# The output projection of a hybrid decoder layer: its weights brought in by halves of their columns, and the last attention head filled with products of two token tiles

## The chip, the cores and the metric

The kernel runs on one core of a Trainium2 chip. The metric is device microseconds of one launch. Before the change three runs gave 1188.72, 1190.84 and 1192.52 us, so the median is 1190.84 us.

## The reference, cut to what matters

One decoder layer on 1024 tokens of width 1024, in float32. Only the middle of it is touched by the change: the mixed output of the two head groups is multiplied by `w_out`, normed and added to the residual.

```python
h = rms_norm(x, norm_mix_pre)
proj = h @ w_in                                  # 2816 columns: u, v of group A; q, k, v of group B
a_out = spatial_gating(ua, va, ...)              # 4 channel groups, 256 columns
b_out = dilated_attention(qb, kb, vb, rel_bias)  # 12 heads, 768 columns
mix = concatenate([a_out, b_out])                # 1024 tokens x 1024
x = x + rms_norm(mix @ w_out, norm_mix_post)     # the part that the change touches
h = rms_norm(x, norm_ffn_pre)
g = gelu(causal_dwconv(h @ w_gate, conv_w, conv_b))
x = x + rms_norm((g * (h @ w_up)) @ w_down, norm_ffn_post)
```

## The kernel before, in words

**Products.** Nearly every matrix product is made of three: each float32 operand is split into a high part (a copy rounded to the format that TensorE takes, on ACT or DVE) and a low part (the difference, on DVE or POOL). `split(hi, lo, src, hi_eng, lo_eng)` at L71 issues the pair, and PE multiplies high by high, high by low and low by high.

**Stages.** First the projection of u, v and the v columns, then the twelve attention heads, then `mix @ w_out` for eight token tiles of 128 tokens (with the norms behind it), then the channel mixer with its gate, up and down products. The attention takes the span from about 130 us to 458 us, the eight tiles of `w_out` from 458 to 545 us.

**One head.** Head h has four groups g of two query tiles. PE makes the scores `s` (L538, L539), DVE adds the bias and takes the row's extreme (`row`, `nm`, L542), ACT takes the exponential (L547), DVE the reciprocal (`rz`, L549), POOL scales the row (L550), PE transposes it (`pt`, L570), ACT and DVE split the transpose (`pth` L574, `ptl` L575), and PE multiplies it by v (`o`, L592). ACT and DVE then put the result into `mix` (`ot` L604, L605). The scores of the next group are issued ahead of the products of this one. Between these steps PE gets fill work from a queue, so many matmuls at each place by the table `FILL_AT`: the q and k projection of the head after next (`qk`, L498), and in the last head (h = 11), which has no head after it, 42 matmuls of `w_out` for token tile 0 (`y`, L649).

**Who orders what.** PE and SP (which issues the DMAs) run in the order in which the code is written. ACT, DVE and POOL get their order from a scheduler at build time. All five run strictly in that order: an instruction that waits holds up all behind it on its engine.

**w_out.** `load_wo(k)` (L624) loads one block of 128 rows by 1024 columns (512 KB) into a raw buffer and splits it into `woh` and `wol`, 512 columns at a time. There are two raw buffers (pool `rp`), which the q and k weights of the heads use as well, so the load of block k+2 waits until block k is split. The tables `WO_HI` and `WO_LO` give the engines by block, and `WO_AT` the place: blocks 0 to 3 in head 10, at groups 0 and 2, blocks 4 and 5 at its group 3, blocks 6 and 7 behind it. `mix_split` (L633) splits the 128 columns of one token tile out of each of the eight `mix` tiles into `ms`, the stationary operand of the `w_out` products. Tile 0 is split in head 10.

**Behind the heads.** At L1112 the last block of `mix` is split for tile 0, its last six matmuls follow, and `wout_end` (L719) takes the sum of squares from both halves of `y`, norms, adds the residual `xb` and norms again. `h2_trans` (L756) then transposes the result of a tile on PE (`hT`, L747), which stands in PE's order behind all of the next tile's matmuls. The banks of PSUM: S three, P two, O one, D two. The two halves of `y` for tile 0 take both banks of D.

Of the kernel before, what the change touches and what calls it, by code (L numbers as in the profile page):

```python
# [52 lines left out]
WQK_HI = 'aa'  # L53
WO_HI = 'dadaddda'
WO_LO = 'pppppppd'
WO_AT = {0: (0, 1), 1: (), 2: (2, 3), 3: (4, 5), 4: (6, 7)}
# [6 lines left out]
def build(tc, x, g1, g2, g3, g4, w_in, ln_g, ln_b, sp_w, sp_b, rel, w_out, w_gate, w_up,  # L63
# [25 lines left out]
    def close_pool(key):  # L89
        cms.pop(key).__exit__(None, None, None)  # L90

    with tc.manual_schedule(engines={ET.PE, ET.SP}), \
# [530 lines left out]

        def load_wo(k):  # L624
            r = raw("wo%d" % k)
            sp.dma_start(r, w_out[k * 128:(k + 1) * 128, :])
            wh = htile("woh%d" % k)
            wl = htile("wol%d" % k)
            for s in (slice(0, 512), slice(512, 1024)):
                split(wh[:, s], wl[:, s], r[:, s], ENG[WO_HI[k]], ENG[WO_LO[k]])  # L630
            WO.append((wh, wl))

# [8 lines left out]

        def wout_mm(i, ks, get):
            def mm(hf, k, j):
                def f():
                    if k == 0 and j == 0:
                        YP[i, hf] = get("y%d_%d" % (i, hf))
                    m = MS[i][1 if j == 2 else 0][:, k]
                    w = WO[k][1 if j == 1 else 0][:, hf * 512:(hf + 1) * 512]
                    pe.matmul(YP[i, hf], m, w, start=k == 0 and j == 0, stop=k == KT - 1 and j == 2)  # L649
                return f  # L650
            return [mm(hf, k, j) for k in ks for hf in range(2) for j in range(3)]

# [6 lines left out]
        for h in range(HEADS):  # L659
# [6 lines left out]
            if h == HEADS - 1:  # L666
                pump(len(fill))
                fill.extend(wout_mm(0, range(KT - 1), bD))
            for g in range(4):
# [16 lines left out]
                if g == 3 and h == HEADS - 2:  # L686
                    pump(len(fill))
                    for k in WO_AT[4]:
                        load_wo(k)
        pump(len(fill))  # L690
        last_pv()
        close_pool("ag")
        close_pool("ag2")
# [421 lines left out]
        load_xb(1)  # L1115
        for f in wout_mm(0, [KT - 1], bD):
            f()
        wout_end(0)
        mt = mix_tiles(1)
        mix_split(1, mt[0], mt[1], range(KT))  # L1120
        for c in range(1, NT):
# [7 lines left out]
            if c == 6:  # L1129
# [3 lines left out]
                hs_sums(0, 2)  # L1133
            for f in wout_mm(i, range(KT), bS if c % 2 else bD):
                f()
# [153 lines left out]
```

## Time and profile before

| | before |
|---|---|
| median of three runs | 1190.84 us (1188.72 to 1192.52) |
| the profiled execution | 1192.9 us, its span 1191.2 us |
| mean granted TensorE clock | 0.996 |
| PE busy | 1162.8 us (98% of the span), 5697 matmuls |
| DVE, ACT, POOL busy | 832.0, 593.1, 351.0 us |
| head 11's first transposes to its last product | 435.05 to 457.9 us |

Of the execution's time, 1.7 us lie outside the span. Columns of a timeline row are the start and the duration in us, the engine, the line, the operation and its operands; a bracket at the end gives the idle time of the engine just before it and who ended that. PE's rows are pipelined and overlap; what a matmul costs is read from the distance between starts.

### The profile page before, as it was taken

The numbers are of one execution on the slowest core, as the hardware profiler recorded it, in microseconds if no ns is written. First come the engines' busy times: TensorE is split into PE (matmuls) and PEld (weight loads), VectorE is DVE, ScalarE is ACT, GpSimd is POOL, SyncE is SP. The second block draws the span as 40 slices with busy tenths as digits, with TensorE's granted clock in tenths as the row PEclk, the third lists the DMA queues.
The fourth block names the chain that finished last, engine by engine and source line by source line (L and its number), as shares of the span: only waits on it lengthen the run. The fifth ranks groups of instructions, "written<-read, shape, count | busy, mean of one in ns | idle before, by whom it ended". The sixth has DMA issues, their size and how long they took to land.

```text
span 1191.2 us, 16581 instructions
## 1 busy us (share of the span) xinstructions
PE 1162.8 (98%) x5697; PEld 975.0 (82%) x5697; DVE 832.0 (70%) x1553; ACT 593.1 (50%) x1233; POOL 351.0 (29%) x356
## 2 busy tenths in 40 slices
PE   8999999999999999998999999999999999999997
PEld 5889978888888878877788888888888888888885
DVE  6842157767777775467997778767777679679666
ACT  6522157676766665467534243433434245445642
POOL 2841023333334473224133313332233310000240
PEclk9999999999999999999999999999999999999999
DMA  5314033443234341341143313333243279334337
GB/s 196 104 47 113 2 83 73 103 108 83 74 78 110 86 131 72 103 164 53 36 133 97 106 65 130 123 108 89 80 133 97 85 279 370 114 98 120 113 108 245
DMA packets 107421, 134.31 MB, mean 113 GB/s; under 512 B 30780, under 2 KB 74312, under 8 KB 107337
## 3 DMA queue, kind: packets, MB, share of 16 engines
q1 hardware_dynamic: 105030, 131.15, 36.1%
q10 hardware_dynamic: 2306, 2.10, 0.5%
q8 instruction: 45, 0.74, 0.3%
q14 instruction: 40, 0.32, 0.1%
HBM read 98.30 MB, written 35.71 MB: 113 GB/s over the span
## 4 chain that ended last, share of the span: by engine, by line
PE 82%; issue 4%; ACT 4%; POOL 4%; DVE 4%; DMA 1%; DVEq 0%; POOLq 0%; ACTq 0%; SPq 0%
PE d L1015 15%; PE qk L498 10%; PE y L649 5%; PE o L592 4%; PE pt L570 4%; PE s L538 2%; PE s L539 2%; PE v L253 2%; PE Bu L876 2%; PE v L254 2%; PE v L255 2%; PE Bu L874 2%; PE Bu L875 2%; PE Au L876 2%; PE Cu L876 2%
## 5 line engine op out<-in xcount | busy, mean ns | idle before, releaser
L1015 PE MATMUL d<-t,s 128*128 128x512 f32 x924 | 210.4, 389 | 0.8 <-DVE t L78 0.8
L1015 PEld LDWEIGHTS d<-t,s 128*128 128x128 f32 x924 | 173.2, 188 | 37.8 <-DVE t L78 1.7
L550 POOL TENSOR_SCALAR row<-row,rz 128x128 f32<-128x128 f32 (+3 forms) x96 | 72.7, 757 | 208.3 <-DVE rz L549 190.7
L547 ACT ACTIVATE row<-row,nm 128x128 f32<-128x128 f32 (+3 forms) x96 | 74.4, 775 | 49.7 <-DVE nm L542 49.5
L575 DVE TENSOR_TENSOR ptl<-pt,pth 128x512 fp32r<-128x512 f32 (+1 forms) x120 | 75.7, 634 | 20.0 <-ACT pth L574 18.7
L649 PE MATMUL y<-woh,ms 128*128 128x512 f32 x256 | 82.8, 396 | 1.0 <-POOL ms L78 0.6
L574 ACT ACTIVATE pth<-pt 128x512 fp32r<-128x512 f32 (+1 forms) x120 | 65.9, 551 | 33.3 <-PE pt L570 31.9
L498 PE MATMUL qk<-hTh,wqh 128*128 128x512 f32 x192 | 81.0, 422 | 0.0
L73 ACT ACTIVATE s<-sf 128x512 fp32r<-128x512 f32 x77 | 48.2, 626 | 63.1 <-PE d L1015 26.3
L498 PE MATMUL qk<-hTl,wqh 128*128 128x512 f32 x192 | 78.7, 410 | 0.0
L498 PE MATMUL qk<-hTh,wql 128*128 128x512 f32 x192 | 76.7, 400 | 0.0
L78 DVE TENSOR_TENSOR s<-sf,s 128x512 fp32r<-128x512 f32 x77 | 57.1, 741 | 21.1 <-ACT s L73 21.0
L570 PE MATMUL pt<-ident,row 128*128 128x128 f32 x432 | 68.3, 275 | 1.1 <-POOL row L550 1.0
L73 ACT ACTIVATE wtg<-tg 128x512 fp32r<-128x512 f32 x44 | 27.4, 632 | 81.4 <-PE Cu L876 67.8
L1030 POOL TENSOR_TENSOR x<-x,g4t 128x512 f32<-128x512 f32 x12 | 18.0, 1516 | 163.4 <-ACT n4m L1040 133.5
L927 DVE SCALAR_TENSOR_TENSOR c<-G,cols,c 128x1023 f32<-128x1023 f32 (+1 forms) x44 | 57.7, 1327 | 6.7 <-ACT c L925 6.7
L542 DVE CUSTOM_DVE_ANT_0 row<-s,bias 128x384 f32<-128x384 f32 (+2 forms) x96 | 49.9, 520 | 17.8 <-PE s L539 12.4
L824 POOL TENSOR_TENSOR tu<-wu 128x512 f32<-128x512 f32 x11 | 16.9, 1537 | 153.6 <-PE Ag L876 74.5
L73 ACT ACTIVATE wtu<-tu 128x512 fp32r<-128x512 f32 x44 | 27.6, 630 | 63.9 <-PE Cg L876 50.8
L570 PEld LDWEIGHTS pt<-ident,row 128*128 128x128 f32 x432 | 51.2, 140 | 10.0 <-POOL row L550 2.0
L649 PEld LDWEIGHTS y<-woh,ms 128*128 128x128 f32 x256 | 47.9, 188 | 11.7 <-POOL ms L78 1.0
L592 PE MATMUL o<-ptl,V 128*128 128x256 f32 x240 | 49.1, 286 | 3.7 <-DVE ptl L575 3.4
(334 smaller groups left out, 3214.1 us busy)
## 6 DMA issues: line engine op xcount, KB each, us to landing
sf<-sD SPq DMA_DIRECT2D x77, 256.0 KB, 2.9
wu<-in_w_up SPq DMA_DIRECT2D x11, 1024.0 KB, 5.1
wd<-in_w_down SPq DMA_DIRECT2D x22, 512.0 KB, 6.9
wg<-in_w_gate SPq DMA_DIRECT2D x10, 1024.0 KB, 6.5
sD<-c SPq DMA_DIRECT2D x30, 256.0 KB, 6.4
gcop<-gd SPq DMA_DIRECT2D x12, 576.0 KB, 4.8
wqk<-in_w_in SPq DMA_DIRECT2D x24, 256.0 KB, 5.8
bias<-gcop SPq DMA_DIRECT2D x12, 512.0 KB, 3.9
```

Source lines behind the costliest of these rows:

```text
L73: act.activation(hi, src, AF.Copy)
L498: pe.matmul(st[hf], w, m, start=k == 0 and j == 0, stop=k == KT - 1 and j == 2)
L547: act.activation(t[:, :w], t[:, :w], AF.Exp, bias=nm, scale=-1.0, accum_out=z)
L550: pool.tensor_scalar(t[:, :w], t[:, :w], rz, 1.0, op0=OP.mult, op1=OP.mult)
L570: pe.transpose(p[:, a * 128:(a + 1) * 128], r[:, jj * 128:(jj + 1) * 128], ident)
L574: act.activation(hi[:, :n], p[:, :n], AF.Copy)
L575: dve.tensor_sub(lo[:, :n], p[:, :n], hi.bitcast(F)[:, :n])
L592: pe.matmul(ov, v, t[:, s], start=j == 0 and x == 0, stop=x == 1 and j == 2 * g + 1, skip_group_check=True)
L649: pe.matmul(YP[i, hf], m, w, start=k == 0 and j == 0, stop=k == KT - 1 and j == 2)
L876: pe.matmul(b, wl, hh, start=False, stop=last and k == 3, skip_group_check=True)
L927: dve.scalar_tensor_tensor(c[:, d:T], g[:, 0:T - d], col(2 - d, f), c[:, d:T], op0=OP.mult, op1=OP.add)
L1015: pe.matmul(b, l, r, start=first and n in FIRST and q == 0, stop=last and n in LAST and q == 2, skip_group_check=True)
```

## The change

`w_out` is brought in by halves of 512 columns (256 KB each). `load_wo(k, hf)` loads and splits half hf of block k. The first halves stand where the whole blocks stood. The second halves are written into the last group of head 11 (blocks 0 to 3) and behind the last head's products (blocks 4 to 7), with their high parts on ACT and their low parts on DVE and POOL in turn. The 42 fill matmuls of the last head become 21 for tile 0 and 21 for tile 1, all on first halves, and so tile 1 of `mix` is split at the start of head 11 instead of behind it (the high parts on ACT, the low parts on POOL). Behind the heads follow the last block's first half for both tiles (6 matmuls), then all of the second half for tile 0 (24), its `wout_end`, and all of the second half for tile 1 (24).

```diff
-WO_HI = 'dadaddda'
-WO_LO = 'pppppppd'
+WO_HI = 'dadaddda', 'aaaaaaaa'
+WO_LO = 'pppppppd', 'dpdpdpdp'
...
-        def load_wo(k):
-            r = raw("wo%d" % k)
-            sp.dma_start(r, w_out[k * 128:(k + 1) * 128, :])
-            wh = htile("woh%d" % k)
-            wl = htile("wol%d" % k)
-            for s in (slice(0, 512), slice(512, 1024)):
-                split(wh[:, s], wl[:, s], r[:, s], ENG[WO_HI[k]], ENG[WO_LO[k]])
-            WO.append((wh, wl))
+        def load_wo(k, hf=0):
+            s = slice(hf * 512, (hf + 1) * 512)
+            r = raw("wo%d_%d" % (k, hf))
+            sp.dma_start(r[:, :512], w_out[k * 128:(k + 1) * 128, s])
+            if hf == 0:
+                WO.append((htile("woh%d" % k), htile("wol%d" % k)))
+            wh, wl = WO[k]
+            split(wh[:, s], wl[:, s], r[:, :512], ENG[WO_HI[hf][k]], ENG[WO_LO[hf][k]])
...
-        def wout_mm(i, ks, get):
+        def wout_mm(i, ks, get, hfs=(0, 1)):
...
-            return [mm(hf, k, j) for k in ks for hf in range(2) for j in range(3)]
+            return [mm(hf, k, j) for k in ks for hf in hfs for j in range(3)]
...
             if h == HEADS - 1:
                 pump(len(fill))
-                fill.extend(wout_mm(0, range(KT - 1), bD))
+                m1 = [mtile("ms1_%d" % s, R).rearrange("p (k c) -> p k c", k=KT) for s in range(2)]
+                mix_split(1, m1[0], m1[1], range(KT - 1), (act, pool))
+                for i in range(2):
+                    fill.extend(wout_mm(i, range(KT - 1), bD, (0,)))
...
+                if g == 3 and h == HEADS - 1:
+                    for k in range(4):
+                        load_wo(k, 1)
         pump(len(fill))
         last_pv()
+        for k in range(4, KT):
+            load_wo(k, 1)
...
-        for f in wout_mm(0, [KT - 1], bD):
+        mix_split(1, m1[0], m1[1], [KT - 1])
+        for i in range(2):
+            for f in wout_mm(i, [KT - 1], bD, (0,)):
+                f()
+        for f in wout_mm(0, range(KT), bS, (1,)):
             f()
         wout_end(0)
-        mt = mix_tiles(1)
-        mix_split(1, mt[0], mt[1], range(KT))
         for c in range(1, NT):
...
-            for f in wout_mm(i, range(KT), bS if c % 2 else bD):
+            for f in wout_mm(i, range(KT), (lambda nm: (bD if nm.endswith("_0") else bS)(nm)) if c == 2 else bS if c % 2 else bD, (1,) if c == 1 else (0, 1)):
                 f()
```

What the scheduler and the buffers make of it is seen in the order of the instructions. PE's own order keeps every row in its place in the last head; only the operands of the fill change. On DVE the cast of block 0 at the start of head 10, which stood behind both score rows of query tile 4, now stands right behind `ptl` of group 0, ahead of the reciprocal of query tile 3 and of those score rows. Three more places count.

The first is ACT, from the transposes of head 11's third group to the first norm of `w_out`'s result. Before:

```order
L574 ACTIVATE pth_2_2_5430<-pt_2_2_5426 128x384
L604 ACTIVATE ot_2_5447<-o_2_5408 64x256
L574 ACTIVATE pth_3_0_5455<-pt_3_0_5450 128x512
L574 ACTIVATE pth_3_1_5465<-pt_3_1_5460 128x512
L574 ACTIVATE pth_3_2_5481<-pt_3_2_5476 128x512
L574 ACTIVATE pth_3_3_5493<-pt_3_3_5489 128x384
L604 ACTIVATE ot_3_5508<-o_3_5459 64x256
L725 ACTIVATE yb_5533,ssb_5534<-y_0_5269 128x512
```

The same place after the change, where `wo_1` is a raw second half:

```order
L574 ACTIVATE pth_2_2_5430<-pt_2_2_5426 128x384
L73 ACTIVATE woh_5125<-wo_1_5527 128x512
L604 ACTIVATE ot_2_5447<-o_2_5408 64x256
L574 ACTIVATE pth_3_0_5455<-pt_3_0_5450 128x512
L574 ACTIVATE pth_3_1_5465<-pt_3_1_5460 128x512
L73 ACTIVATE woh_5131<-wo_1_5531 128x512
L73 ACTIVATE woh_5206<-wo_1_5535 128x512
L574 ACTIVATE pth_3_2_5481<-pt_3_2_5476 128x512
L574 ACTIVATE pth_3_3_5493<-pt_3_3_5489 128x384
L604 ACTIVATE ot_3_5524<-o_3_5459 64x256
L73 ACTIVATE woh_5212<-wo_1_5539 128x512
L734 ACTIVATE yb_5592,ssb_5593<-y_0_5269 128x512
```

The copies of blocks 4 (`woh_5125`), 5 (`woh_5131`) and 6 (`woh_5206`) now stand ahead of work on which PE waits in the last group.

The second place is POOL in head 11, after the change, between the scaling of query tile 4's row and that of tile 5's:

```order
L550 TENSOR_SCALAR row_4_5279<-row_4_5279,rz_4_5292 128x640
L78 TENSOR_TENSOR ms_1_5217<-mix_790,ms_0_5216 128x128
L78 TENSOR_TENSOR ms_1_5217<-mix_791,ms_0_5216 128x128
L78 TENSOR_TENSOR ms_1_5217<-mix_1588,ms_0_5216 128x128
L78 TENSOR_TENSOR ms_1_5217<-mix_2242,ms_0_5216 128x128
L78 TENSOR_TENSOR ms_1_5217<-mix_2901,ms_0_5216 128x128
L78 TENSOR_TENSOR ms_1_5217<-mix_3560,ms_0_5216 128x128
L78 TENSOR_TENSOR ms_1_5217<-mix_4219,ms_0_5216 128x128
L78 TENSOR_TENSOR ms_1_4859<-mix_4893,ms_0_4858 128x128
L78 TENSOR_TENSOR ms_1_5217<-mix_4893,ms_0_5216 128x128
L550 TENSOR_SCALAR row_5_5295<-row_5_5295,rz_5_5308 128x768
```

Before, one such row (`ms_1_4859`) stood between the two. The seven rows of tile 1 that ACT copies ahead of them (`ms_0_5216`) stand together on ACT behind `ot` of group 0 and ahead of `pth` of the second group's first transposes (`pth_1_0`), and the copy of block 7's first half stands there ahead of query tile 4's exponential.

The third place is SP's queue at the end, after the change, each row with what it waits for (Pool and DVE: the split that frees the raw buffer; DMAHW: earlier transfers):

```order
L628 DMA wo_1_5504<-in_w_out 128x512 [waits DMAHW7_49,DMAHW1_49,Pool_49]
L628 DMA wo_1_5508<-in_w_out 128x512 [waits DMAHW2_49,DMAHW0_49,DVE_49]
L628 DMA wo_1_5512<-in_w_out 128x512 [waits DMAHW1_49,DVE_49]
L628 DMA wo_1_5516<-in_w_out 128x512 [waits DMAHW2_49,Pool_49]
L628 DMA wo_1_5527<-in_w_out 128x512 [waits DMAHW5_49,DMAHW3_49,DVE_49]
L628 DMA wo_1_5531<-in_w_out 128x512 [waits DMAHW6_49,DMAHW5_49,DVE_49]
L628 DMA wo_1_5535<-in_w_out 128x512 [waits DMAHW4_49,Pool_49]
L628 DMA wo_1_5539<-in_w_out 128x512 [waits DMAHW6_49,Pool_49]
L725 DMA xb_5554<-in_x 128x1024
L1123 DMA g2t<-in_norm_mix_post 128x1024 [waits PE_49]
```

These eight loads are new rows, ahead of the residual `xb` and the gain `g2t`. The fifth (block 4) waits for DVE's split of block 2, and the sixth (block 5) waits for DVE's split of block 4: it takes the buffer that block 4 has just left, not that of block 3, whose split is POOL's.

## The prediction, made before the changed kernel was run

> **What bounds the kernel now.** I read the page's busy shares first, then the chain that ended last, then who PE waits for in the stretch that the change touches.
>
> ```profile
> span 1191.2 us, 16581 instructions
> PE 1162.8 (98%) x5697; PEld 975.0 (82%) x5697; DVE 832.0 (70%) x1553; ACT 593.1 (50%) x1233; POOL 351.0 (29%) x356
> PE 82%; issue 4%; ACT 4%; POOL 4%; DVE 4%; DMA 1%; DVEq 0%; POOLq 0%; ACTq 0%; SPq 0%
> ```
>
> PE is busy for 98% of the span and carries 82% of the chain. The change leaves PE its matmuls, as many and as large, so it can win only what PE waits, and every wait that it adds is time. The next view is PE's waits from 400 to 560 us: engine and line, what was waited for, the sum in us, how often, the longest.
>
> ```profile
> PE o L592 <- DVE ptl L575: 2.9, 2, 1.9
> ...
> PE y L649 <- POOL ms L78: 0.6, 1, 0.6
> PE y L649 <- DVE Q L513: 0.4, 1, 0.4
> PE pt L570 <- POOL row L550: 0.4, 1, 0.4
> PE s L538 <- DVE nm L542: 0.2, 1, 0.2
> ```
>
> The two rows left out are waits of `hT` in the last tiles, where both kernels have the same instructions. What the change can reach is the rest: 4.5 us, and 1.0 of that (the other `ptl` wait, 2.9 less 1.9) lies at 406.66 us (first row of the next fence), ahead of the first load's landing. That leaves 3.5 us. So the gain has a ceiling near 0.3%, about what a measurement of this kernel can tell from no change, and the question is what waits come in.
>
> **The change part by part.** The profiled execution took 1192.9 us, 2.06 over the median; terms are against it.
>
> **A, waits that go.** The largest wait has a load behind it: behind PE's row at 432.44 stands DVE's row of the timeline, and behind that the load in the chain.
>
> ```profile
> 406.66 0.45 PE L592 MATMUL o<-ptl,V 128*128 128x256 f32 x2 [1.04 <-DVE ptl L575]
> ...
> 432.44 0.51 PE L592 MATMUL o<-ptl,V 128*128 128x256 f32 x2 [1.90 <-DVE ptl L575]
> 430.96 0.43 DVE L77 CAST woh<-wo 128x512 fp32r<-128x512 f32 x1 [2.11 <-DMA wo<-in_w_out]
> 425.19 5.74 DMA wo<-in_w_out
> ```
>
> DVE stood 2.11 us for block 5, whose 512 KB took 5.74 us, and `ptl` stood behind it. A half is smaller and POOL splits only seven pieces in head 10, where it split 14, so the load starts sooner as well. I take the whole 1.90 away, and with POOL's lighter queue the `row` wait (0.4) and the `Q` wait (0.4), which stand behind it: −2.7. What is late next is the scaling of a row, priced in B and C. Block 5 was slower than the median block (4.8, below), so in a run near the median A may be smaller by 5.74 − 4.8 = 0.9; that widens the upper side.
>
> **B, the first cast in head 10.** It now stands on DVE right behind `ptl` of group 0, with the reciprocal of query tile 3 and both score rows of tile 4 queued behind it, for which POOL, ACT and PE wait in turn. How long does half a block take? The transfer view gives median us from issue to landing:
>
> ```profile
> wo<-in_w_out SPq DMA_DIRECT2D x8, 512.0 KB, 4.8
> x<-in_x SPq DMA_DIRECT2D x7, 512.0 KB, 3.6
> x<-in_x SPq DMA_DIRECT2D x2, 256.0 KB, 2.7
> sf<-sD SPq DMA_DIRECT2D x77, 256.0 KB, 2.9
> ...
> DMA to landing us min/median/max: 3.8/4.8/5.7
> ```
>
> The last row is of the eight blocks alone: 3.8 to 5.7 us. A 256 KB load took 2.7 to 2.9 elsewhere in this trace. The program issues, casts and uses here:
>
> ```profile
> 406.51 0.87 SPq L626 DMA_DIRECT2D wo<-in_w_out  x2
> 409.10 0.55 DVE L575 TENSOR_TENSOR ptl<-pt,pth 128x384 fp32r<-128x384 f32 x1
> 410.07 0.16 DVE L549 RECIPROCAL rz<-z 128x1 f32<-128x1 f32 x1 [0.41 <-ACT row L547]
> 411.31 0.76 DVE L77 CAST woh<-wo 128x512 fp32r<-128x512 f32 x2
> 411.54 0.61 PE L570 MATMUL pt<-ident,row 128*128 128x128 f32 x4
> L78 POOL TENSOR_TENSOR wol<-wo,woh x14: 1279/1300/1438, 411.8 to 441.9; 128x512 fp32r<-128x512 f32 x14
> 410.40 0.69 POOL L550 TENSOR_SCALAR row<-row,rz 128x512 f32<-128x512 f32 x1 [1.19 <-DVE rz L549]
> ```
>
> The half lands no sooner than 406.51 + 2.7 = 409.2, and no later than 411.3, since the whole block's cast ran at 411.31 without a wait. I take the middle, 410.25, since eight whole blocks took 1.2 us more than the `x` loads of their size (4.8 and 3.6), and the half's share of such a delay is open. The cast of 0.4 then ends at 410.65, where the reciprocal began at 410.07: 0.6 late, and the score rows with it. On POOL the first subtraction (1.30) now stands ahead of query tile 3's scaling, which ends at 410.65 + 1.30 + 0.69 = 412.65, with about 0.1 of hand-over 412.75. PE comes to its transposes at 411.54 + 0.6 = 412.15 and waits 0.6 more. B is **+1.2**. With a landing at 409.2 only the subtraction counts (411.4 + 0.7 against 411.54: +0.5); at 411.3 the sum is 413.75 − 411.54 = +2.2.
>
> The Trainium skill (DMA: Bandwidth & Descriptors, section "Anatomy of one DMA — SWDGE (gpsimd) path") gives a DMA that GpSimd issues a fixed part of about 2.0 us and the rest by bytes, which speaks against halving, since sixteen loads pay the fixed part where eight did; by it 256 KB would take an estimated 2.6 us, and the sum below would be some 0.8 lower. The trace agrees (2.7 against 3.6 us for the two sizes of `x`), for loads that SP issues.
>
> **C, head 11's first half.** ACT copies seven blocks of `mix` for tile 1 ahead of `pth` of the second query group, and POOL makes nine low parts between two scalings where it made one. Unit prices come from tile 1's split behind the heads in before, and the slack from the rows where the copies will stand:
>
> ```profile
> 460.24 1.70 ACT L73 ACTIVATE ms<-mix 128x128 fp32r<-128x128 f32 x8
> 441.07 0.60 ACT L574 ACTIVATE pth<-pt 128x512 fp32r<-128x512 f32 x1
> 442.40 0.69 DVE L575 TENSOR_TENSOR ptl<-pt,pth 128x512 fp32r<-128x512 f32 x1
> 460.62 4.48 POOL L78 TENSOR_TENSOR ms<-mix,ms 128x128 fp32r<-128x128 f32 x8 [7.88 <-ACT ms L73]
> 445.33 0.91 POOL L550 TENSOR_SCALAR row<-row,rz 128x768 f32<-128x768 f32 x1
> ```
>
> Seven copies are 7 × 1.70 / 8 = 1.5 us. `pth` ended at 441.67 and `ptl` began at 442.40, so 0.73 of it is slack: +0.8. On POOL eight more low parts are 8 × 0.56 = 4.5 us, less two subtractions of 1.30 that leave the head's start: the scaling at 445.33 moves by up to 1.9. Most of that lies beside ACT's delay and beside PE's fill; I take +0.4 of it. C is **+1.2**, with ends at 0 (ACT and POOL have run ahead) and 0.8 + 1.9 + 0.4 (block 7's copy ahead of an exponential) = 3.1.
>
> **D, the second halves in the last group.** There are two raw buffers, and eight loads go through them in a row. On DVE the low part of block 2 stands behind the second piece of query tile 7's row, and ACT's copies of blocks 5 and 6 stand ahead of `pth` for the third piece of its transposes, so PE's last products wait for two loads in series:
>
> ```profile
> 449.15 0.74 DVE L542 CUSTOM_DVE_ANT_0 row<-s,bias,nm 128x512 f32<-128x512 f32 x1
> 457.09 0.40 PE L592 MATMUL o<-pth,V 128*128 128x256 f32 x2
> L73 ACT ACTIVATE woh<-wo x6: 618/622/624, 413.3 to 442.1; 128x512 fp32r<-128x512 f32 x6
> L78 DVE TENSOR_TENSOR wol<-wo,woh x2: 678/706/735, 443.0 to 443.7; 128x512 fp32r<-128x512 f32 x2
> ```
>
> Low part of block 2 0.71, load of block 4 2.8 (between 2.7 and 2.9), copy 0.62, low part 0.71, load of block 5 2.8, copies of blocks 5 and 6 1.24, `pth` 0.60, hand-overs some 0.3 (seven of 0.04, an estimate from the rows' distances): 9.8 us. Before, from the row's end at 449.89 to those products at 457.09 passed 7.2 us. That is +2.6, and +0.4 for the last `ptl` behind another low part of 0.71, part of it under PE's fill. But C's delay is in the same 7.2 us for the most part, since row 7's scores are issued ahead of the products that C holds up: I take 0.9 of C's 1.2 off. D is **+2.1**; ends 0 (the loads start ahead of the row's end and the chain is hidden) and +4.1 (loads of 3.8).
>
> **E, behind the heads.** `hT` of tile 0 stands behind 24 matmuls, where 48 stood. The norm chain that it must cover, in tile 1 of before:
>
> ```profile
> 462.24 9.37 PE y L649 x40
> 475.10 0.35 ACT L161 ACTIVATE n_1m<-ssb,n_1m 128x1 f32<-128x1 f32 x1
> 475.53 0.55 POOL L166 TENSOR_TENSOR n_1r<-n_1m,half 128x1 f32<-128x1 f32 x1 [1.33 <-ACT n_1m L161]
> 480.96 0.75 DVE L735 TENSOR_SCALAR xb<-yb,n_1r 128x1024 f32<-128x1024 f32 x1 [2.18 <-POOL n_1r L154]
> ```
>
> From 475.53 to 481.71 are 6.2 us, ahead of them the square of the second half and the statistic, some 1.1 (0.35 for the last step, the rest the square): 7.3. A matmul costs 9.37 / 40 = 0.234, so the cover is 5.5 or 5.6 us: +1.9 of waiting. The wait of 0.6 for POOL's low parts of tile 1 goes, since those are in head 11: E is **+1.3**. Its ends are 0.3 (the first half's square out of the way early) and 2.3. Everything behind is the same order, later.
>
> Sum: −2.7 + 1.2 + 1.2 + 2.1 + 1.3 = **+3.1**. The profiled execution would become 1196.0, and the median 1190.84 + 3.1 = **1193.9**.
>
> **The rivals.**
> *The loads stay hidden.* ACT is busy 50% and POOL 29%, so copies may slip into their gaps and C and D cost nothing: −2.7 + 1.2 + 1.3 = −0.2, 1190.6 us. For it: eight copies of weights and seven of `mix`, each under 0.63 us, fit in an engine that idles half the time. Against it: these queues are strict, and the copies stand ahead of `pth`. Without any new wait at all the sum would be −3.3 (A and the 0.6), 1187.5.
>
> *Slower by the loads in series.* Four half-loads lie on the path: one each in B and C (block 7's copy) and two in D. If a half takes 3.8 us, as the quickest whole block did, where I took 2.8, each adds 1.0: +7.1, 1197.9. It becomes clearly slower from 0.1 us on per load (0.4 in all), since the forecast stands just under that bound. For it: whole blocks took 4.8 here where `x` took 3.6. Against it: the two sizes of `x`.
>
> *The clock falls.* The windows show that PE's gaps can cost clock as well; PE busy is the first number behind the length, the granted clock stands third from the end.
>
> ```profile
> 430.00:435.00 5.00, 3.10 (x22) 2.73 (x21) 3.10 (x8) 2.18 (x4) 3.42 (x4) 1.00 0.01 2
> 555.00:560.00 5.00, 3.48 (x21) 2.71 (x20) 3.93 (x5) 4.17 (x12) 1.03 (x2) 1.00 0.01 3
> ...
> 565.00:570.00 5.00, 4.24 (x13) 3.28 (x14) 5.00 (x11) 3.00 (x3) 1.31 (x1) 0.72 0.00 0
> ```
>
> The window with the 1.90 wait kept 1.00, but thin work from 555 us was followed by 0.72 for 5 us: 5 × 0.28 = 1.4 us. If D's waits gather in one stretch that comes on top: +4.5, 1195.3. The Trainium skill (TensorE: Matmul & The Clock Gate, section "What's actually happening") has the clock fall after an idle window of about 3.4 us; by it no single wait priced here is long enough.
>
> **How the numbers follow.** Forecast 0.48 (its own range 1192 to 1195.5, from the choices in C, D and E), loads hidden 0.20, loads in series 0.24, clock 0.08. The range of 1189 to 1198.5 takes in all four and leaves out the ends where several bounds meet. 0.3% is 3.6 us: faster means under 1187.3, where only the case without new waits comes near, 0.08. Slower means over 1194.4: all of the series, most of the clock, some 0.35 of the forecast's own: 0.24 + 0.06 + 0.17 = 0.47. The rest is 0.45.
>
> **What would show it.** A: no `o` wait of 1.9 near 432. B: an idle of DVE's first cast near 410 that ends with the load. C: POOL's nine low parts in one row ahead of a scaling, and PE waiting for `pth` or `row` near 441 to 447. D: ACT's copies of blocks 5 and 6 idle until their loads land, and PE's last `o` waiting for `pth` past 457. E: `hT` of tile 0 waiting near 2 us for `xb`. I am wrong if ACT's copies in the last group find their halves landed, or if halves take as long as blocks.

## The result, and the profile after

| | before | after |
|---|---|---|
| median of four runs each | 1191.68 us (1188.72 to 1192.87) | 1202.47 us (1200.05 to 1202.88) |
| ratio, 95% interval | | 1.0083 [1.0069, 1.0097] |
| the profiled execution, its span | 1192.9, 1191.2 us | 1202.14, 1200.3 us |
| mean granted TensorE clock | 0.996 | 0.993 |

The change makes the kernel about 9.9 us slower (0.0083 × 1191.68; by the interval 8.2 to 11.6). The sign is the one forecast, the size is three times the forecast and lies outside its range. One execution, the profiled one of e16, was disturbed (1229.66 us at a granted clock of 0.894), and its trace is not read below. The span and the busy times of the page after:

```profile
span 1200.3 us, 16590 instructions
PE 1167.0 (97%) x5697; PEld 978.5 (82%) x5697; DVE 835.6 (70%) x1543; ACT 597.3 (50%) x1242; POOL 342.6 (29%) x357
```

PE has as many matmuls as before, and its share of the span is one point lower: new waits. But PE's busy time also grew, by 4.2 us, with the same matmuls. A matmul that runs at a lower clock takes longer (eight transposes `hT` take 1.06 us at a clock of 1.00 and 1.77 across a fall to 0.50, in rows below), so part of the loss is no wait at all: after has two stretches at half clock more than before, 3.41 us each, from 477.32 and from 1180.47. PE's waits from 400 to 480 us after the change (engine, line and tile, what was waited for, the sum in us, how often, the longest):

```profile
PE o L592 <- ACT pth L574: 4.0, 3, 2.6
PE o L592 <- DVE ptl L575: 2.1, 5, 1.0
PE hT L756 <- DVE xb L744: 2.0, 1, 2.0
PE s L538 <- DVE nm L542: 1.2, 2, 0.8
PE pt L570 <- POOL row L550: 0.5, 1, 0.5
...
```

The 1.90 behind block 5 is gone (a wait of 0.61 for `pth` at 429.24 is new in head 10), and ACT's `pth`, which PE did not wait for at all before, now leads. Where the time came in is read from the starts of one and the same PE row in two traces. These rows of after stand where in before stood the rows that start at 406.95, 441.89, 452.72, 458.01 and 483.23 us:

```profile
406.59 0.51 PE L570 MATMUL pt<-ident,row 128*128 128x128 f32 x3
440.44 0.49 PE L570 MATMUL pt<-ident,row 128*128 128x128 f32 x3
453.71 0.28 PE L570 MATMUL pt<-ident,row 128*128 128x128 f32 x1
462.58 0.45 PE L650 MATMUL y<-woh,ms 128*128 128x512 f32 x1
490.58 1.03 PE L756 MATMUL hT<-ident,xb 128*128 128x128 f32 x8
```

The first two rows are 0.36 and 1.45 us early, the third 0.99 late, and so on; the steps between them are the stages of the table, in us (hundredths by unrounded starts). The same two kernels were profiled once more later (experiments e13 and e5), and the last column is the mean of the two profiles of after less the mean of the two of before:

| stage (starts in before) | predicted | after | after again | before again | difference of the means |
|---|---|---|---|---|---|
| to the last group of head 9 (406.95) | 0 | −0.35 | −1.72 | +0.26 | −1.2 |
| head 10 (to 441.89) | A + B, −1.5 | −1.10 | −0.88 | −0.88 | −0.6 |
| head 11, first half (to 452.72) | C, +1.2 | +2.44 | +2.51 | +0.15 | +2.4 |
| its last group (to 458.01) | D, +2.1 | +3.58 | +3.65 | −0.01 | +3.6 |
| to the transposes of tile 1 (483.23) | E, +1.3 | +2.79 | +2.75 | +0.02 | +2.8 |
| to the last stage (1153.44) | 0 | −0.69 | −0.77 | −0.72 | −0.4 |
| the rest, to the end | 0 | +2.46 | +3.17 | +2.55 | +1.5 |

The four stages that the change touches sum to 8.2 us. The others sum to about nothing, and before against itself shows how far they move: its second profile was 2.55 us longer behind 1153 us, where PE's waits for `t` sum to 2.4 us in place of 0.8 and a stretch of 3.41 us at half clock follows (from 1171.73) that its first profile does not have. Both profiles of after have such a stretch in the tail too. So the tail of after is not put down to the change.

### The profile page after: what moved, and what is told of

Its sections match the earlier page's. It is cut to its first block, busy times and chain, and to the rows that moved or that the text cites. A ratio compares the mean times of both kernels' runs of the same rounds, so it can differ in the third digit from the quotient of the medians.

```text
span 1200.3 us, 16590 instructions
## 1 busy us (share of the span) xinstructions
PE 1167.0 (97%) x5697; PEld 978.5 (82%) x5697; DVE 835.6 (70%) x1543; ACT 597.3 (50%) x1242; POOL 342.6 (29%) x357
## 4 chain that ended last, share of the span: by engine, by line
PE 83%; DVE 5%; issue 4%; ACT 4%; POOL 2%; DMA 2%; SPq 0%; DVEq 0%; POOLq 0%; ACTq 0%
PE d L1024 15%; PE qk L498 10%; PE y L650 4%; PE o L592 4%; PE pt L570 4%; PE s L538 2%; PE s L539 2%; PE v L253 2%; PE Bu L885 2%; PE v L254 2%; PE v L255 2%; PE Bu L883 2%; PE Bu L884 2%; PE Au L883 2%; PE Cu L883 2%
## 5 line engine op out<-in xcount | busy, mean ns | idle before, releaser
L592 PEld LDWEIGHTS o<-pth,V 128*128 128x128 f32 x240 | 43.6, 188 | 12.6 <-ACT pth L574 5.5
```

The costliest lines, as they stand in the source:

```text
L592: pe.matmul(ov, v, t[:, s], start=j == 0 and x == 0, stop=x == 1 and j == 2 * g + 1, skip_group_check=True)
```

## The experiments

Ratios are to the kernel before on the same chip. e1 to e4, e6, e7 and e9 to e11 ask what each part costs, e5 and e13 how far a profile repeats, e14 and e15 which engine holds C and D, e12, e16 and e17 whether the change can be made to win. Diffs are against the changed kernel unless said.

### E: the transposes of tile 0 (e1)

```diff
-            for f in wout_mm(i, ...):
+            for n, f in enumerate(wout_mm(i, ...)):
+                if c == 2 and n == 18:
+                    h2_trans(TO[0], bP)
                 f()
...
-                h2_trans(TO[c - 1], bP)
+                if c > 1:
+                    h2_trans(TO[c - 1], bP)
```

> The changed kernel, with the transposes of tile 0's normed result put behind 18 matmuls of tile 2, not ahead of all 48 of them. Theory (the cover of 24 matmuls is too short, and PE's wait behind it pulls the granted clock down): the wait of 2.04 us for xb goes, and the windows from 476 to 484 us, granted 0.67 and 0.91, go back to 1.00, which gives 4 x 0.33 + 4 x 0.09 = 1.7 us: 3.7 us less than the changed kernel, about 1.0052 of the kernel before. Rival 1 (the clock falls because of the thin stretch of 455 to 462 us, not of this wait): only the 2.0 us go, 1.0066. Rival 2 (the norm chain holds up what comes next on DVE and ACT anyway): nothing is won, 1.0083.

Measured: 1197.31 us, 1.0037 [1.0025, 1.0049]. After's PE row with the wait, then two windows (length, then busy us of PE, PEld, DVE, ACT and POOL, then the granted clock):

```profile
477.12 1.77 PE L756 MATMUL hT<-ident,xb 128*128 128x128 f32 x8 [2.04 <-DVE xb L744]
```

```profile
473.91:477.32 3.41, 1.36 (x8) 0.85 (x7) 2.17 (x10) 3.22 (x11) 0.92 (x2) 1.00 0.71 219
477.32:480.73 3.41, 3.41 (x13) 3.02 (x12) 1.73 (x3) 2.83 (x11) 1.97 (x5) 0.50 0.24 94
```

The wait is 2.04 us, and right behind it PE runs at half clock for 3.41 us. 3.41 us at 0.50 do the work of 1.7: the wait costs another 1.7. In e1 the same transposes, 18 matmuls later:

```profile
479.34 1.03 PE L756 MATMUL hT<-ident,xb 128*128 128x128 f32 x8
```

```profile
476.00:480.00 4.00, 4.00 (x23) 3.36 (x22) 1.74 (x4) 2.33 (x11) 2.86 (x6) 1.00 0.57 186
```

No bracket, full clock. The stage to 483.23 went from +2.79 to −1.09, 3.9 us, where the wait alone was 2.0. So E is real, and it has a second part nearly as large as the first, which is clock.

### D: the second halves' buffers (e2)

```diff
-            r = raw("wo%d_%d" % (k, hf))
-            sp.dma_start(r[:, :512], w_out[...])
+            if hf == 0 or k % 2 == 0:
+                RWO.append(raw("wo%d_%d" % (k, hf)))
+            r = RWO[-1][:, :512] if hf == 0 or k % 2 == 0 else RWO[-1][:, 512:]
+            sp.dma_start(r, w_out[...])
```

> The changed kernel, with the second halves of blocks 2j and 2j+1 put into the two halves of one raw buffer, so that four half-loads can be under way in the same memory, and no load waits for the split just ahead of it. Theory (two raw buffers put the loads in series, and pth in the last group waits for the copies that wait for them): PE's waits of 2.6 and 0.3 us near 461 go for the most part, 2.5 to 3.3 us less than the changed kernel, 1.0055 to 1.0062 of the kernel before. Rival (the copies on ACT's strict queue cost by their own time, whenever they land): eight copies of 0.63 us stay where they are, and at most 1 us is won, 1.0075 or above.

Measured: 1198.76 us, 1.0051 [1.0039, 1.0063]. The last group lost 1.19 in place of 3.58, but head 11's first half 4.60 in place of 2.44: together 5.8 against 6.0. The row of ACT's copy ahead of the last `pth` of the third group says why:

```profile
452.99 0.63 ACT L73 ACTIVATE woh<-wo 128x512 fp32r<-128x512 f32 x1 [1.54 <-DMA wo<-in_w_out]
```

The scheduler puts the copies of loads that can start sooner in sooner places as well, here in the third group, and ACT stood 1.54 us for a landing there; PE's wait behind it was 2.06 us. More buffers moved the wait and did not remove it. No new wait of PE is left in e2's last group: its 1.19 is clock, a stretch at 0.50 from 456.08 to 459.49, right behind the wait.

### C: tile 1's split put into head 10 (e3)

The seven blocks that stood at the start of head 11 are split at group 1 of head 10.

```diff
-                mix_split(1, m1[0], m1[1], range(KT - 1), (act, pool))
...
+                    if g == 1:
...
+                        mix_split(1, m1[0], m1[1], range(KT - 1), (act, pool))
```

> The changed kernel, with the seven finished blocks of mix split for tile 1 in group 1 of head 10, not at the start of head 11. Theory (seven copies on ACT ahead of pth and eight low parts on POOL ahead of a row's scaling cost the 2 us by which PE falls back between 440 and 446 us): these go, but head 10 takes 1.5 us of ACT and 3 us of POOL instead, beside a fill of 11 matmuls: 0.5 to 2 us less than the changed kernel, 1.0066 to 1.0079. Rival (the loss between 440 and 446 is that of the weights' copies and low parts there): nothing is won in head 11, and head 10 loses 1 us, 1.009.

Measured: 1199.99 us, 1.0066 [1.0054, 1.0078]. Head 11's first half went from +2.44 to +1.48, and head 10 from −1.10 to +0.27: what one won the other lost, since head 10 has no room for the copies either. So 1.0 of C goes with the seven copies, and 1.5 stays without them. Yet the stage to 483.23 lost only 1.12, with the same 2.04 us wait, and no half clock:

```profile
477.67 1.06 PE L757 MATMUL hT<-ident,xb 128*128 128x128 f32 x8 [2.04 <-DVE xb L745]
```

```profile
475.83:479.24 3.41, 1.57 (x11) 1.50 (x12) 1.42 (x3) 3.38 (x15) 2.28 (x5) 1.00 0.78 263
479.24:482.66 3.42, 3.42 (x16) 2.82 (x15) 2.64 (x3) 1.44 (x7) 0.61 (x2) 1.00 0.00 0
```

The wait is as long and lies otherwise in time; the section on the hardware takes it up.

### Halves alone (e4)

The kernel before, with each block loaded by two DMAs of 512 columns (against before):

```diff
-            sp.dma_start(r, w_out[k * 128:(k + 1) * 128, :])
...
             for s in (slice(0, 512), slice(512, 1024)):
+                sp.dma_start(r[:, s], w_out[k * 128:(k + 1) * 128, s])
                 split(...)
```

> The kernel before, with nothing but this: each block of w_out comes by two loads of 512 columns into the two halves of its raw buffer, and each split waits for its own half. Theory (the wait for block 5's load goes by the earlier first half, and the fill and the second halves' place are what cost): the 1.9 us near 432 shrink to below 1, and the sum lies between 0 and 2 us less than before, 0.9983 to 1.0000. Rival (sixteen loads or their landing are what cost): slower than before, 1.002 or above.

Measured: 1197.34 us, 1.0042 [1.0030, 1.0055], slower where my theory had it no slower. Head 10 alone lost 3.47. PE's waits from 400 to 440 us, then who waited for the tile `wo` (the sum, how often), and one of DVE's casts:

```profile
PE o L592 <- DVE ptl L575: 1.7, 3, 1.0
PE s L538 <- DVE nm L542: 1.5, 2, 0.8
...
```

```profile
  DVE woh L77: 3.1, 6
  ACT woh L73: 2.3, 1
```

```profile
416.83 0.43 DVE L77 CAST woh<-wo 128x512 fp32r<-128x512 f32 x1 [0.53 <-DMA wo<-in_w_out]
```

A half that is expected sooner gets its cast placed sooner, in front of score rows. DVE stands for landings six times, 3.1 us in all, and ACT once, 2.3 us; before, DVE stood three times, 3.3 us in all, and ACT never. PE's waits in the stretch sum to 5.5 us in place of 3.9, and these 1.6 are about half of the 3.47. The other half is clock, a stretch at 0.50 from 432.78 to 436.19, shown in the last section. Halving the loads is no gain in itself. That the change comes out ahead in head 10 because it holds half of the bytes and of the splits there is argued, not shown.

### Before again (e5) and after again (e13)

> The kernel before, unchanged, with a profile of its own. Of the 9.1 us by which the spans of the two profiled executions differ, 2.5 us came up behind 1169 us, where both kernels have the same order. Theory (the loads of the residual there land by chance, and a stretch at half clock of 3.4 us follows where PE has stood long enough in a window): in another execution of the kernel before, the wait of PE for t near 1171 us may be 0.6 or 2 us, and the count of half-clock stretches may differ by one to two; up to 569 us its PE rows stand within 1.5 us of the first profile's. Rival (the changed kernel's tail is slower for a reason of its own): this profile repeats the first within 0.3 us behind 1160 us.

> The changed kernel again, unchanged, with a profile of its own. Theory: up to 450 us its PE rows stand within 1 us of the first profile's; the last of 16 pieces of block 6's load, which came 1.4 us behind the others there, lands with them, so that PE's wait for pth near 461 is 1.2 us and not 2.6, while the median stays at 1.006 to 1.009 of the kernel before. Rival (that straggler is the program's own): the wait is 2.6 us again.

Measured: 1194.14 us, 0.9995 [0.9981, 1.0009], and 1202.06 us, 1.0077 [1.0065, 1.0089]. Their stages are in the table above. Two things came of them. In before again PE's wait behind block 5 was shorter:

```profile
431.81 0.50 PE L592 MATMUL o<-ptl,V 128*128 128x256 f32 x2 [1.21 <-DVE ptl L575]
```

And D repeats to a tenth, with the slow load in it. The chain that ended last, from 450 to 462 us, in after and in after again (start, us, what):

```profile
450.35 2.54 DMA wo<-in_w_out
...
452.92 0.64 ACT woh L73
...
453.58 1.12 DVE wol L78
454.71 0.33 SPq L628
...
455.13 4.66 DMA wo<-in_w_out
...
459.82 0.64 ACT woh L73
...
461.09 0.69 DVE ptl L575
```

```profile
449.28 2.60 DMA wo<-in_w_out
...
454.06 4.73 DMA wo<-in_w_out
```

Block 4 landed in 2.54 us, block 6 in 4.66. The records of the single transfers show 15 of block 6's 16 pieces landed by 458.35 and the last at 459.79. A fetch of instructions, one packet of 16 KB, ran from 456.89 to 458.28, and the last transfers of the load start one behind the other from 458.27 on. In the transfer view of after, 455 to 460 us:

```profile
q8 instruction: 1, 0.02, 1.7%
```

1.7% of 16 engines over 5 us are 1.4 us of one engine. The late piece is 1.44 us late. In after again, e1 and e9 the load that ended the chain took 4.73, 4.57 and 4.68 us, in e15 3.79, and in all five profiles the last piece landed 1.5 to 1.6 us after the fetch had ended. Where the schedule put the loads elsewhere against that fetch, the load in the chain (block 5's) took 3.27 (e3) and 2.88 (e14), and in e17 no load is in that chain. That it was chance, which I had thought possible, fell: it belongs to the place in the program. No run moved the fetch by itself, and the records name no engine, so that the fetch held the piece back rests on these times.

### D by the code's place (e6, e7)

e2's pairs of buffers, with the splits of blocks 4 to 7 written behind the last products (`load_wo` gives them back as a function); e7 is this with e1's transposes.

```diff
+        ws = [load_wo(k, 1, True) for k in range(4, KT)]
         last_pv()
-        for k in range(4, KT):
-            load_wo(k, 1)
...
         mix_split(1, m1[0], m1[1], [KT - 1])
+        for f in ws:
+            f()
```

> The changed kernel with the raw halves in pairs as in e2, and with the splits of the last four second halves (their copies on ACT, low parts on DVE and POOL) written behind the last head's products; the loads stay where they are in SP's queue. Theory (it is the place of the copies in ACT's strict queue ahead of pth that costs, not the time of the loads): PE's waits for pth and ptl behind 449 us, 3 to 4.5 us in the changed kernel and in e2, fall below 1 us, and the four splits hide beside the first 18 matmuls of the second half: 2.5 to 4 us less than e2, 1.002 to 1.003 of the kernel before. Rival (the loads are late): the second half's matmuls of blocks 4 to 7 wait for the copies instead, and the time is e2's, 1.005.

> e6 with e1's later transposes of tile 0. Theory (the two costs are apart, so the gains add): 3 to 5 us less than e6, 0.998 to 1.000 of the kernel before: then the idea of the change would no longer cost, nor win. Rival (both wait for the same late chain on ACT): the gain over the better of e1 and e6 is below 1 us, 1.002 or above.

Measured: 1201.14 us, 1.0053 [1.0037, 1.0068], and 1196.91 us, 1.0025 [1.0014, 1.0036]. e6 tested nothing of what it was made for: on ACT the copies stayed in the places that they had in e2, though they were written later.

```profile
454.64 0.63 ACT L73 ACTIVATE woh<-wo 128x512 fp32r<-128x512 f32 x1 [1.59 <-DMA wo<-in_w_out]
455.18 0.47 ACT L574 ACTIVATE pth<-pt 128x384 fp32r<-128x384 f32 x1
```

Head 11's first half lost 4.72, as in e2. e7 shows that E's loss goes whatever else is there (stage −1.11).

### D by a dependency (e10, e11)

The same, but the late copies multiply by a column of ones that is computed from the last head's result, so that they can't run earlier; e11 is this with e1's transposes.

```diff
+        if one is not None:
+            act.activation(hi, src, AF.Copy, scale=one)
...
         last_pv()
+        dve.tensor_scalar(one, mixT[KT - 1][:, 1023:1024], 0.0, 1.0, op0=OP.mult, op1=OP.add)
+        for f in ws:
+            f(one)
```

> e6 left its four copies in their old places on ACT, so here they are forced behind: the raw halves in pairs as in e2, and the copies of the second halves of blocks 4 to 7 multiply by a column of ones that DVE makes from the last entry of the last head's result, so that none can stand ahead of pth. Theory (place in ACT's strict queue costs): PE's waits for pth and ptl between 449 and 463 us fall from 2.5 to 3.5 us to below 1 us, and the low parts follow in time for blocks 4 to 7: 2.5 to 4 us less than e2 and e6, 1.002 to 1.003 of the kernel before. Rival (the splits are only moved): PE waits for them in the second half's matmuls near 463 to 466 us, and less than 1 us is won.

> e10 with e1's later transposes of tile 0. Theory (both costs are apart): another 3 to 4 us less than e10, 0.999 to 1.000 of the kernel before; what is left against it is head 11's first half (+2 us) less the wait for block 5 that is gone (about 1 us net in head 10). Rival (the late splits hold up the norm of tile 0 in turn): 1.002 or above.

Measured: 1199.07 us, 1.0044 [1.0030, 1.0058], and 1194.91 us, 1.0019 [1.0010, 1.0027]. In the last group e10 and e11 lost nothing against before (−0.07, −0.06), with the same bytes loaded through the same buffers as in e6, and head 11's first half lost 1.76 and 2.00 in place of e6's 4.72. D is the copies that stand ahead of `pth`, not the loads. What it cost in place of that is a row of e10's waits from 440 to 480 us:

```profile
PE y L657 <- DVE wol L80: 1.7, 1, 1.7
```

PE now waits 1.7 us for a low part of a second half, once, behind the heads.

### The first loads sooner (e9)

Blocks 0 and 1's first halves are issued at the end of head 9; their splits stay where they were.

```diff
+                if g == 3 and h == HEADS - 3:
+                    for k in (0, 1):
+                        load_raw(k)
```

> The changed kernel, with the loads of the first halves of blocks 0 and 1 issued at the end of head 9, ahead of the bias load; the splits stay where they are. Theory (the first cast waits for its half, with the score rows behind it): PE's wait of 0.8 us for nm near 410.8 and part of the 0.5 us for the row behind it go, 0.8 to 1.3 us less than the changed kernel, 1.007. Rival (the order of the cast, not its load, costs): 0.5 us or less is won, 1.008.

Measured: 1201.55 us, 1.0061 [1.0045, 1.0077]. Head 10 came to −2.25 in place of −1.10, so the first cast's wait is worth 1.15, about the 1.2 that B had. The last group lost 4.19, more than in after: its wait of 2.63 us for `pth` fell into one window of 3.41 us with PE busy for 0.78, and half clock followed from 459.12. In after the same wait, 2.62 us, lay across two windows, busy for 1.53 and 2.35, and cost no clock. Of the gain nothing certain reaches the total.

### C and D: which engine holds them (e14, e15)

e14 lets tile 1's seven copies wait, by the same device as in e10, for `pth` of the second group's last transposes. e15 gives all low parts of the second halves to POOL.

```diff
-                mix_split(1, m1[0], m1[1], range(KT - 1), (act, pool))
...
                 last_pv = tpv(h, g, FILL_AT.get(h, FILL)[g])
+                if h == HEADS - 1 and g == 1:
+                    mix_split(1, m1[0], m1[1], range(KT - 1), (act, pool), ones("one1", PTL[h, 1, 1]))
```

```diff
-WO_LO = 'pppppppd', 'dpdpdpdp'
+WO_LO = 'pppppppd', 'pppppppp'
```

> The changed kernel, with tile 1's seven copies of finished mix blocks forced behind pth of the second group's last transposes (they multiply by a column of ones that DVE makes from that pth); the low parts on POOL follow them, so the row of query tile 5 is scaled ahead of them. What PE loses between its transposes at 441.9 and 445.9 us was 2.1 us in the changed kernel. Theory (0.9 and 0.5 of it are ACT's copies ahead of pth, 0.65 is DVE's low part of block 0's second half ahead of query tile 6's score rows): 0.6 to 0.8 us of loss are left there, and the median is 1 to 1.5 us under the changed kernel's, 1.007 of the kernel before, unless the copies now hold up query tile 6's row. Rival 1 (POOL's nine low parts cost): the same here, but also 0 in e15. Rival 2 (the fill's matmuls of tile 1): 2.1 us stay.

> The changed kernel, with the low parts of all second halves on POOL, none on DVE. Theory: DVE's share of the loss between 441.9 and 450.4 us goes (0.65 at the scores of query tile 6, 0.4 to 0.7 at ptl of group 2), ACT's 1.4 us stays; POOL's longer queue (1.3 us each) delays the second halves: the load of block 5 then waits for POOL. So 0.5 to 1.5 us less than the changed kernel, or nothing where POOL gives it back in the last group: 1.007 to 1.008. Rival (POOL was what costs in head 11): slower than the changed kernel, 1.010.

Measured: e14 1197.35 us, 1.0040 [1.0024, 1.0056]; e15 1198.55 us, 1.0048 [1.0031, 1.0064]. After, ACT and then PE:

```profile
440.56 1.51 ACT L73 ACTIVATE ms<-mix 128x128 fp32r<-128x128 f32 x7
441.98 0.57 ACT L574 ACTIVATE pth<-pt 128x512 fp32r<-128x512 f32 x1
...
443.75 0.93 ACT L547 ACTIVATE row<-row,nm 128x768 f32<-128x768 f32 x1
```

```profile
442.61 0.51 PE L592 MATMUL o<-pth,V 128*128 128x256 f32 x2 [0.74 <-ACT pth L574]
443.33 0.51 PE L592 MATMUL o<-ptl,V 128*128 128x256 f32 x2 [0.22 <-DVE ptl L575]
...
445.54 0.50 PE L538 MATMUL s<-Kh,Q 128*128 128x512 f32 x1 [0.43 <-DVE nm L542]
```

Three waits follow from seven copies: `pth` 0.74, `ptl` behind it 0.22, and through DVE's queue the next score row 0.43. In e15 the same PE rows wait 0.74, 0.22 and 0.45 us, so DVE's low parts have no share in it. In e14, with the copies behind `pth`:

```profile
440.03 0.60 ACT L583 ACTIVATE pth<-pt 128x512 fp32r<-128x512 f32 x1
...
443.71 2.15 ACT L73 ACTIVATE ms<-mix,one 128x128 fp32r<-128x128 f32 x7
```

```profile
441.14 0.39 PE L602 MATMUL o<-pth,V 128*128 128x256 f32 x2
442.10 0.50 PE L602 MATMUL o<-ptl,V 128*128 128x256 f32 x2 [0.56 <-DVE ptl L584]
...
444.06 0.50 PE L540 MATMUL s<-Kh,Q 128*128 128x512 f32 x1 [0.17 <-DVE nm L544]
```

The wait for `pth` is gone, and the three sum to 0.73 in place of 1.39. But head 11's first half as a whole lost 2.53 in e14, as much as after's 2.44: other waits came in its place, 0.46 and 0.16 at 449.74 and 450.37. So the copies' place made the wait of 0.74, and moving them behind `pth` won nothing in C. What e14 won, it won in the last group, which lost 0.46 in place of 3.58: by the order that the scheduler chose there, the loads of blocks 5 and 6 landed at 454.79 and 455.46, where after's landed at 457.75 and 459.79, and ACT came to their copies, ahead of the last group's second and third `pth`, at 454.81 and 455.83. e15's lost 2.30: POOL's splits give the buffers back at other times, and the load that ended last took 3.79 us in place of 4.66.

### Together (e12, e16, e17)

e12 is e11 with e9's early loads. e16 is e12 with e14's copies. e17 is the changed kernel with e1's transposes, e9's loads and e14's copies, and no pairs.

> e11 with e9's early loads of the first two halves. Theory: 1 to 2 us less than e11, as e9's profile stood 2.2 us ahead of the changed kernel's at the end of head 10: 0.998 to 0.999 of the kernel before, the first version that does not cost. Rival (that lead is lost again behind head 10): e11's time.

> e12 (early first loads, raw pairs, late copies of blocks 4 to 7, later transposes of tile 0), with two steps more: the late copies hang on pth of the last group rather than on the last result, so they start some 2 us earlier, and tile 1's copies stand as in e14. Theory: the wait of 1.7 us for wol near 463 falls below 0.5, and 1 to 1.4 us go in head 11: 2 to 3 us less than e12, 0.998 of the kernel before, faster. Rival (the copies hold up query tile 6's row and ot in their new places): e12's time, 1.0005, or above.

> The changed kernel with the three steps that gained by themselves: tile 0's transposes later (e1), tile 1's copies behind pth (e14), the first two loads early (e9); raw buffers, copies of the second halves and their engines as in the change. Theory (the gains add): PE's rows stand 1 to 2 us ahead of the kernel before's from the second tile's transposes on, and the time is 0.998 to 0.999 of it, the first version that wins. Rival (the loads of the last second halves wait again, since they start on other terms, and meet the 1.4 us by which a piece of a load came late): 1.001 to 1.003.

Measured: 1193.41 us, 1.0005 [0.9996, 1.0014]; 1193.62 us, 1.0004 [0.9994, 1.0015]; 1192.89 us, 0.9999 [0.9987, 1.0011]. All three stand level with before: the loss is recovered, and nothing is won. The two longest of PE's waits in e17 between 440 and 480 us:

```profile
PE o L602 <- DVE ptl L584: 0.6, 2, 0.4
PE o L602 <- DVE mix L615: 0.5, 1, 0.5
```

No `hT`, no `pth`, no `y`. Its stages are −2.40 in head 10, +2.54 and +0.25 in head 11 and −1.13 behind it: C is the part that none of the three steps took away.

## Why the prediction was right and wrong

**The ceiling held.** The waits that the change could remove were put near 0.3%. The best version of it, e17, stands level with before: nothing won that a measurement could tell.

**A was right, and leaned on one slow load.** The 1.90 is gone from after. But before again waited 1.21 there, as the text said of a run nearer the median, so head 10 won 0.6 on the means and not 1.5.

**B was right.** The first cast waited for its load, and the two waits behind it sum to 0.77 + 0.48 = 1.25 us (0.2 of it stood there before) against 1.2. DVE's row, then PE's:

```profile
409.99 0.43 DVE L77 CAST woh<-wo 128x512 fp32r<-128x512 f32 x1 [0.69 <-DMA wo<-in_w_out]
```

```profile
410.87 0.44 PE L538 MATMUL s<-Kh,Q 128*128 128x384 f32 x1 [0.77 <-DVE nm L542]
412.51 0.55 PE L570 MATMUL pt<-ident,row 128*128 128x128 f32 x3 [0.48 <-POOL row L550]
```

**C had the mechanism and half of the size:** 2.4 for 1.2. The failing step is "`pth` ended at 441.67 and `ptl` began at 442.40, so 0.73 of it is slack: +0.8". The first wait, 0.74, is that 0.8. The sum stopped there. The same delay goes on to `ptl` (0.22) and to the score row behind it on DVE (0.43). The sum also has no term for the second halves of blocks 0 to 3, whose copies the scheduler put into this half of the head as well (on ACT at 443.23, 444.67, 448.05 and 451.24). Without the seven copies of tile 1, 1.5 of the 2.4 were still there (e3), and with the copies in another place all of it (e14). No run took the second halves out of this place, so where the 1.5 comes from stays open. The share of POOL (+0.4) was not tested by itself.

**D had the mechanism, and one load was mis-sized:** 3.6 for 2.1. The two loads in series, the halves of block 4 with 2.54 and 2.60 us (2.8 assumed) and the copies ahead of `pth` are in the chain as forecast. The failing step is "load of block 5 2.8, copies of blocks 5 and 6". Block 6's load, taken to land beside block 5's, landed 1.44 us after its other pieces, and 3.58 − 1.44 = 2.1. The rival of loads in series, at 1197.9, came nearest by its total and was wrong in its reason: a half under way alone took 2.5 to 2.6 us and not 3.8, and only block 6's took more than that.

**E was right as a wait:** 2.04 us for 1.9, and +1.1 for +1.3 where the clock holds (e3, e15).

**The clock is what the sum left out:** 1.7 us. The rival "the clock falls" priced it well (1.4), but gave it 0.08 and looked for it behind D's waits; in the change it came behind E's, and behind waits for `pth` only in e2, e6, e7 and e9. The step that failed is that the sum has no term for a fall behind a single wait, E's 1.9 above all: it went by the window with the 1.90 wait in before, which kept 1.00, and by the sentence that no single wait priced there is long enough. The Trainium skill (TensorE: Matmul & The Clock Gate, section "What's actually happening") has the clock fall after an idle window of about 3.4 us. The trace agrees on the window, 3.41 us, and differs on idle: PE was busy for 1.36 us of the window ahead of the fall. The measurement decides: a wait of 2.04 us was enough. The text should have priced E's wait with and without a fall.

So on the means C fell short by 1.2, D by 1.5, A and B by 0.9, and the clock by 1.7, and E was 0.2 too dear: 5.1 us on top of 3.1 is the 8.2 of the table. The ratio's 9.9, with an interval from 8.2 to 11.6, leaves room for more that no stage of the change shows. One small sum of the prediction is off in itself: with loads of 2.6 us its own terms give 0.7 less in B and 0.4 less in D, so 1.1 and not 0.8. Nothing else hangs on it.

## What to carry to other kernels

Bytes moved off a stage in front come back as copies on a strict queue: what counts is the first instruction behind each copy on which PE waits, and then everything behind that one as well, not the busy share of the engine. Price a load on the path by its latest piece, and a wait of PE by its length and by the window of the clock that it can fall into. Where a scheduler orders an engine, a step is moved by a dependency; where its code stands decides little.

## What the hardware showed that was not expected

**The clock's window.** Behind the first 30 us, every stretch of half clock in the traces lasts 3.41 us, but for one that runs into the end of each. In after the starts of two of them, 477.32 and 572.89, lie 28 such windows apart (95.57 / 3.41 = 28.03). The second is in before too:

```profile
563.77:567.18 3.41, 1.42 (x6) 1.05 (x6) 2.50 (x4) 1.74 (x3) 2.19 (x2) 1.00 0.00 0
567.18:570.59 3.41, 3.41 (x10) 2.72 (x9) 3.41 (x8) 2.53 (x3) 0.00 (x0) 0.50 0.00 0
```

So the clock goes by windows of a fixed raster. Where the raster lies differs from run to run, and no run set it. PE's busy time within a window counts, but does not settle it alone. Behind the first 30 us of these traces half clock followed every full-clock window with PE busy for less than 1.44 of 3.41 us (1.36 in after, 1.37 in e13, 1.42 in before), and none with more than 1.88. In between it went both ways: it followed 1.53 (e6), 1.66 (e2) and 1.88 (e4), and not 1.50 (e9), 1.57 (e3), 1.78 (e15) or, at 456.84 in after, 1.53. What else decides there is open. The window of e4:

```profile
429.37:432.78 3.41, 1.88 (x9) 1.18 (x8) 2.90 (x9) 1.40 (x4) 3.33 (x3) 1.00 0.33 115
432.78:436.19 3.41, 3.41 (x16) 3.22 (x15) 1.72 (x3) 0.60 (x1) 3.26 (x4) 0.50 0.01 2
```

What a wait costs thus hangs on how it lies against the windows: with the same wait of 2.04 us, E's stage lost 1.1 us where 0.2 to 0.4 of the wait lay in the window ahead (e3, e15), and 2.8 where it lay in one (after). Six of the nine profiles with the short cover had the fall.

**A fetch of instructions and the last piece of a load.** In five profiles (after, e13, e1, e9, e15) the fetch of 16 KB began 1.3 to 1.9 us after block 6's half had been issued. The last of its 16 pieces then landed 1.3 to 1.6 us behind the one before it, and 1.5 to 1.6 us after the fetch had ended. In four of the five that load took 4.57 to 4.73 us, where a half under way alone took 2.5 to 2.6. In e14 and e17 the fetch began 2.5 us after the issue, when the first pieces were landing, and no piece came late. No run moved the fetch alone.
